# The 32-row substitution of an RWKV-7 mixer: its matrix moved to PSUM, its products laid along contiguous rows

## Chip, cores and metric

The kernel runs on 1 core of one Trainium2 chip. The metric is device microseconds of one execution, the median of several runs.

## The reference

A decoder trunk of two layers over 512 tokens of width 1024. Layer 0 mixes its tokens with an RWKV-7 recurrence (8 heads of 64) beside a spatial gate, layer 1 with latent attention; each then attends to 256 memory tokens and passes through a mixture of 32 experts. Only the recurrence matters here:

```python
def rwkv7_recurrence(r, w, k, v, kk, a):
    def step(state, inp):
        r_t, w_t, k_t, v_t, kk_t, a_t = inp
        sa = jnp.einsum('bhvk,bhk->bhv', state, -kk_t)
        state = (state * w_t[:, :, None, :]
                 + sa[..., None] * (kk_t * a_t)[:, :, None, :]
                 + v_t[..., None] * k_t[:, :, None, :])
        return state, jnp.einsum('bhvk,bhk->bhv', state, r_t)
    ...
    _, y = lax.scan(step, state0, xs)
```

The kernel computes it in chunks of 128 tokens. Within a chunk the steps are a triangular system with a unit diagonal, and its 128x128 matrix has to be inverted: 4 chunks times 8 heads give 32 such matrices.

## The kernel before, in words

`mixer` (L717) holds layer 0's mixer. Two generators share its first part. `prep` (L831) makes the matrices and inverts them. `filler` (L991) runs the projections that need no inverse: `take_g`, `take_r`, `shifted` into `vv`, and `spatial`. The lines after them advance the two in turn, and a scheduler then fixes the order on each engine; every engine works through its own queue in that order.

A projection (`proj_cm`, `proj_tm`; lines L212 to L214) is a row of 128x512 matmuls in three passes, since each operand is split into a high and a low part: ACT casts the high part (L218), POOL subtracts the low part (L219). Its sum in PSUM is picked up by `shifted` (L760 on ACT, then L761 on DVE, which frees the PSUM tile), and for `take_r` by a product `bt` (L941 on DVE) that feeds the small matmuls `pbn` (L946).

In `prep`, PE makes all 32 matrices (L871) and ACT copies them to `Aab` (L873). The four 32x32 blocks of each diagonal are inverted together, on DVE alone. Partition 32x+u holds, for block x, row u, and the free axis the 32 matrices:

1. L877 copies the diagonal blocks into `tsum`, transposed in the free axis and multiplied by a triangular mask; four instructions, one per block of 32 partitions. L878 transposes them in 32x32 blocks into `dd`.
2. L881 to L883, for i from 1 to 31, is the substitution: 31 dependent pairs, a product of i by i elements and a sum along its last axis. Row i of the inverse `tr` comes from all rows before it.

```python
for i in range(1, 32):
    V.tensor_tensor(prod[:, 0:i, 0:i], tr[:, 0:i, 0:i].rearrange("p j c -> p c j"),
                    dd[:, None, 0:i, i].to_broadcast([P, i, i]), op=ALU.mult)
    V.tensor_reduce(tr[:, i, 0:i], prod[:, 0:i, 0:i], axis=AX.X, op=ALU.add)
```

   `tr`, `prod` and `dd` have rows of 32 elements, 128 bytes. The product reads `tr` down its columns, 128 bytes from element to element, and `dd` as well; it writes `prod` with the summed index last, so the sum reads contiguous elements.
3. L890 and L892 transpose the result into `TT` (in the tile `h`) and `tsum`, while L887 copies it on ACT. PE then joins the blocks to 64 and to 128 rows (`pC` L900, `pT` L910, and L922 to L931), with ACT and DVE copies between.

The loop yields at every second step, so DVE's queue holds `r`, `bt`, `bon` and four `vv` of the filler between the pairs. All of this uses one PSUM pool with four tiles of tag "a" (prep) and four of tag "b" (filler). When both generators are done the second part of the mixer runs chunk by chunk, then cross attention, then the experts, whose weights come from HBM through SP's queue (L104).

Of the kernel before, what the change touches and what calls it, by code (L numbers as in the profile page):

```python
# [15 lines left out]
ALU = mybir.AluOpType  # L16
AX = mybir.AxisListType
# [3 lines left out]
P = 128  # L21
# [323 lines left out]
def out_proj(k, pool, sp, w, yh, yl, gb, tags="ab", order=(0, 1), route=False, fine=False):  # L345

    nc = k.nc
    V = nc.vector
    st = [k.ln_stats(pool, i) for i in range(NT)]
    for half in range(2):  # L350
        s = slice(half * 512, (half + 1) * 512)

        def consume(i, ps):
            V.scalar_tensor_tensor(k.h[:, i, s], k.h[:, i, s], ALPHA, ps, op0=ALU.mult, op1=ALU.add)
            V.bn_stats(st[i][:, half], k.h[:, i, s])
            if half == 1:
                scale = k.ln_scale(pool, st[i], f"ln_{i}")
                if route:
                    k.router.step(i, scale, *gb)
                else:  # L360
                    k.layer_norm(k.h[:, i, :], scale, *gb)

        yield from proj_tm(k, sp, w, half * 512, yh, yl, NT, tags[half], consume, by_token=(half == 1), order=order, fine=fine)
# [353 lines left out]
def mixer(k):  # L717
    nc, tc, A, c = k.nc, k.tc, k.A, k.cst
    V, S_, G_, E = nc.vector, nc.scalar, nc.gpsimd, nc.tensor
# [4 lines left out]
    with ExitStack() as st:  # L724
# [18 lines left out]
        with ExitStack() as s1:  # L743
# [3 lines left out]
            xh = pool.tile([P, KD, T], F32R, name="xh")  # L747
            xl = pool.tile([P, KD, T], F32R, name="xl")
            mt1 = pool.tile([P, MIXA.shape[1]], F32, name="mixa")
            scan, selT, tri, dmask, sel = (mt1[:, o:o + n] for o, n in ((0, 512), (512, 512), (1024, P), (1152, 32), (1184, 2)))  # L750
            omu = pool.tile([P, 14], F32, name="omu")
            oka = pool.tile([P, 4], F32, name="oka")
            wa = pool.tile([P, T], F32, name="wa", tag="wa")
# [77 lines left out]
            def prep():  # L831
# [24 lines left out]
                Aab = pool.tile([P, 32, P], F32, name="Aab")  # L856
                b8 = pool.tile([P, 2048], F32, name="b8")
                t8 = pool.tile([P, 2048], F32, name="t8")
                tsum, dd = (b8[:, o:o + 1024].rearrange("p (i u) -> p i u", u=32) for o in (0, 1024))
                tr, prod = (t8[:, o:o + 1024].rearrange("p (i u) -> p i u", u=32) for o in (0, 1024))  # L860
                G_.memset(tr, 0.0)
                G_.memset(t8[:, 0:1024:33], 1.0)
                for x in range(1, 4):
                    G_.memset(TT[32 * x:32 * x + 32, 0:32 * x, :], 0.0)
                for p in range(4):
                    pj = [k.psum("a", name="pab") for j in range(2)]
                    for q in range(NT):
                        qs = slice(q * P, (q + 1) * P)
                        for j in range(2):
                            r = slice(64 * j, 64 * j + 64)  # L870
# [3 lines left out]
                    yield  # L874
                for x in range(4):
                    r = slice(32 * x, 32 * x + 32)
                    V.tensor_tensor(tsum[r].rearrange("p i u -> p u i"), Aab[r, :, r], dmask[r, None, :].to_broadcast([32, 32, 32]), op=ALU.mult)  # L877
                V.transpose(b8[:, 1024:], b8[:, 0:1024])  # L878
                yield
                for i in range(1, 32):  # L880
                    V.tensor_tensor(prod[:, 0:i, 0:i], tr[:, 0:i, 0:i].rearrange("p j c -> p c j"),  # L881
                                    dd[:, None, 0:i, i].to_broadcast([P, i, i]), op=ALU.mult)
                    V.tensor_reduce(tr[:, i, 0:i], prod[:, 0:i, 0:i], axis=AX.X, op=ALU.add)  # L883
                    if i % 2:
                        yield

                S_.copy(prod, tr.rearrange("p i c -> p c i"))  # L887
                for x in range(4):
                    r = slice(32 * x, 32 * x + 32)
# [5 lines left out]
                for n in range(2):  # L895
                    ps = k.psum("a", name="pC")
                    for u in range(16):
                        for h in (0, 64):
                            r, ri = slice(h + 32, h + 64), slice(h, h + 32)
# [91 lines left out]
            def filler():  # L991
# [3 lines left out]
                yield from spatial()  # L995

            pr, fl = prep(), filler()
            next(pr)
            for n in (2, 2, 2, 2):
# [11 lines left out]
        with ExitStack() as s2:  # L1011
# [146 lines left out]
            op = out_proj(k, tp, sp, A["ab_w_out"], y, None, ln, tags="aa", order=(1, 0), fine=True)  # L1158
# [895 lines left out]
def build(nc, tc, A, out, phases):  # L2054
    k = B(nc, tc, A, out)
    with ExitStack() as st:
# [18 lines left out]
        for ph in phases:  # L2075
# [17 lines left out]
            elif ph[0] == "xamoe":  # L2093
                with ExitStack() as rs:
                    cross_attention(k, ph[1], rs)
                    fill = None
                    if ph[1] == 0:
                        fill = early_keys(k, 1, "g")
                    moe(k, rs, ph[1], ph[2], fill)
            elif ph[0] == "xa":  # L2100
                with ExitStack() as rs:
                    cross_attention(k, ph[1], rs)
            elif ph[0] == "mix":
                mixer(k)
            elif ph[0] == "mla":
                mla(k)
            elif ph[0] == "store":
                if k.kept:
                    k.kept.close()
                nc.sync.dma_start(out.rearrange("(i p) d -> p i d", p=P), k.h)  # L2110
# [40 lines left out]
```

## Time and profile before

| | us |
|---|---|
| median of 3 runs (1974.23 to 1977.72) | 1976.72 |
| the profiled execution | 1979.66 |
| its span, first to last instruction | 1977.9 |

The profiled execution is 2.9 us above the median, and 1.8 us of it lie outside the span. PE is busy for 91% of the span, DVE for 48%, ACT for 27%, POOL for 14%. "Busy" adds up instructions; an idle stretch of an engine is printed in square brackets at the instruction that ended it, with the engine, tile and line that released it.

### The profile page before, as it was taken

The numbers are of one execution on the slowest core, as the hardware profiler recorded it, in microseconds if no ns is written. First come the engines' busy times: TensorE is split into PE (matmuls) and PEld (weight loads), VectorE is DVE, ScalarE is ACT, GpSimd is POOL, SyncE is SP. The second block draws the span as 40 slices with busy tenths as digits, with TensorE's granted clock in tenths as the row PEclk, the third lists the DMA queues.
The fourth block names the chain that finished last, engine by engine and source line by source line (L and its number), as shares of the span: only waits on it lengthen the run. The fifth ranks groups of instructions, "written<-read, shape, count | busy, mean of one in ns | idle before, by whom it ended". The sixth has DMA issues, their size and how long they took to land. (4 is left out here: it accounts for less than half of the span.)

```text
span 1977.9 us, 23921 instructions
## 1 busy us (share of the span) xinstructions
PE 1799.2 (91%) x9222; PEld 1105.9 (56%) x9222; DVE 956.1 (48%) x2129; ACT 530.0 (27%) x992; POOL 280.4 (14%) x278
## 2 busy tenths in 40 slices
PE   8778998999979999999896999999979999998895
PEld 5567877878844344434336866678863334433332
DVE  5686456855553233323236566575573233333325
ACT  6313313344221111111122555434322111111110
POOL 3532433410110000000022100130020000000002
PEclk9886889999979999999998999999989999999998
DMA  5220105472889999999995200234679999999992
GB/s 187 65 64 23 54 1 203 128 234 78 330 311 414 420 419 419 420 420 419 420 369 171 88 22 22 86 112 155 227 311 360 420 419 419 420 420 420 421 418 102
DMA packets 126022, 514.69 MB, mean 260 GB/s; under 512 B 15520, under 2 KB 49472, under 8 KB 77264
## 3 DMA queue, kind: packets, MB, share of 16 engines
q1 hardware_dynamic: 115152, 486.60, 62.3%
q0 software_dynamic: 7056, 18.12, 2.8%
q10 hardware_dynamic: 3696, 8.41, 1.1%
q8 instruction: 74, 1.21, 0.2%
q14 instruction: 44, 0.36, 0.1%
HBM read 506.19 MB, written 14.70 MB: 263 GB/s over the span
## 5 line engine op out<-in xcount | busy, mean ns | idle before, releaser
L1756 PE MATMUL pu<-wu,xT 128*64 128x512 f32 x1024 | 240.7, 594 | 21.9 <-DMA wu<-in_moe_w_up_dram 21.8
L1756 PE MATMUL pg<-wg,xT 128*64 128x512 f32 x1024 | 232.8, 601 | 1.6 <-DMA wg<-in_moe_w_gate_dram 1.6
L1782 PE MATMUL py<-wd,hh 128*64 128x512 f32 x1024 | 230.4, 599 | 0.0
L1789 DVE SCALAR_TENSOR_TENSOR wy<-py,tab,wy 128x512 fp32r<-128x512 f32 x64 | 45.5, 747 | 285.7 <-ACT wy L1788 285.4
L1762 DVE TENSOR_TENSOR hh<-hh,pu 128x512 f32<-128x512 f32 x32 | 22.0, 688 | 322.0 <-PE pu L1756 322.0
L1756 PEld LDWEIGHTS pu<-wu,xT 128*64 128x64 f32 x1024 | 77.4, 137 | 178.1 <-issue 131.3
L1796 PE MATMUL pc<-wy,wc 128*128 128x512 f32 x480 | 139.8, 422 | 27.3 <-DVE h L1806 27.3
L1745 ACT ACTIVATE xT<-px,ch 128x128 f32<-128x128 f32 x128 | 48.2, 457 | 424.7 <-PE px L1738 404.2
L1756 PEld LDWEIGHTS pg<-wg,xT 128*64 128x64 f32 x1024 | 77.6, 139 | 149.4 <-issue 130.6
L1806 DVE TENSOR_TENSOR h<-h,pc 128x512 f32<-128x512 f32 x240 | 151.0, 680 | 8.6 <-PE pc L1796 8.6
L1782 PEld LDWEIGHTS py<-wd,hh 128*64 128x64 f32 x1024 | 71.4, 138 | 135.1 <-issue 130.5
L1796 PEld LDWEIGHTS pc<-wy,wc 128*128 128x128 f32 x480 | 81.6, 189 | 85.9 <-DVE h L1806 50.0
L1720 POOL DMA_INDIRECT xg<-rows,idx x32 | 33.5, 1046 | 532.6 <-PE px L1738 513.2
L1726 ACT ACTIVATE xg<-xg 128x1024 f32<-128x1024 f32 x32 | 39.7, 1240 | 245.4 <-DMA xg<-rows,idx 245.4
L218 ACT CAST wh<-wt 128x1024 fp32r<-128x1024 f32 x50 | 51.8, 1050 | 107.1 <-PE ptm L214 61.5
L219 DVE TENSOR_TENSOR wl<-wt,wh 128x1024 fp32r<-128x1024 f32 x37 | 47.9, 1302 | 58.4 <-ACT wh L218 57.9
L212 PE MATMUL ptm<-wh,oh 128*128 128x512 f32 x192 | 75.6, 394 | 0.0
L213 PE MATMUL ptm<-wl,oh 128*128 128x512 f32 x192 | 75.0, 391 | 0.0
L214 PE MATMUL ptm<-wh,ol 128*128 128x512 f32 x192 | 75.0, 390 | 0.0
L212 PE MATMUL pcm<-xh,wh 128*128 128x512 f32 x144 | 61.7, 429 | 7.6 <-ACT xh L218 7.2
L214 PE MATMUL pcm<-xh,wl 128*128 128x512 f32 x144 | 60.5, 420 | 0.5 <-DVE wl L219 0.5
L213 PE MATMUL pcm<-xl,wh 128*128 128x512 f32 x144 | 60.0, 416 | 0.2 <-DVE xl L219 0.2
(565 smaller groups left out, 3432.1 us busy)
## 6 DMA issues: line engine op xcount, KB each, us to landing
wg<-in_moe_w_gate_dram SPq DMA_DIRECT2D x128, 1024.0 KB, 19.8
wu<-in_moe_w_up_dram SPq DMA_DIRECT2D x128, 1024.0 KB, 20.2
wd<-in_moe_w_down_dram SPq DMA_DIRECT2D x124, 1024.0 KB, 19.9
wr<-in_ab_w_in_dram SPq DMA_DIRECT2D x8, 1024.0 KB, 5.7
wr<-in_xa_wkv_dram SPq DMA_DIRECT2D x8, 1024.0 KB, 10.8
wt<-in_xa_wkv_dram SPq DMA_DIRECT2D x8, 1024.0 KB
wr<-in_xa_wq_dram SPq DMA_DIRECT2D x8, 1024.0 KB, 8.2
wt<-in_xa_wo_dram SPq DMA_DIRECT2D x8, 1024.0 KB
```

The lines of the kernel that those rows point to most:

```text
L212: nc.tensor.matmul(out, lh, rh, start=start, stop=False)
L213: nc.tensor.matmul(out, lh, rl, start=False, stop=False)
L214: nc.tensor.matmul(out, ll, rh, start=False, stop=stop)
L218: k.nc.scalar.copy(hi, src)
L219: (eng or k.low()).tensor_tensor(lo, src, hi.bitcast(F32), op=ALU.subtract)
L1726: self.k.nc.scalar.activation(x[:, :D], x[:, :D], AF.Identity, scale=x[:, D:D + 1], bias=x[:, D + 1:D + 2])
L1745: r = nc.scalar.activation(self.xT[:, kk, :], pk, AF.Identity, scale=gk, bias=bk)
L1756: nc.tensor.matmul(ps[j * M:(j + 1) * M, :], self.xT[:, half * 4 + kk, j * M:(j + 1) * M], w[j][:, kk, :], start=(half == 0 and kk == 0), ...
L1782: nc.tensor.matmul(py[n][j * M:(j + 1) * M, :], self.hT[:, half * 2 + kk, j * M:(j + 1) * M], w[j][:, kk, n * 512:(n + 1) * 512], start=(h ...
L1789: nc.vector.scalar_tensor_tensor(yl, py[n], self.tab()[:, 1:2], yh.bitcast(F32), op0=ALU.mult, op1=ALU.subtract)
L1796: self.k.nc.tensor.matmul(ps, self.C[:, i * P:(i + 1) * P], y, start=start and not last, stop=last)
L1806: k.nc.vector.tensor_add(k.h[:, i, s], k.h[:, i, s], pc)
```

## The change

The substitution keeps its arithmetic and changes its layout. `dd` moves to PSUM: two ACT copies (L883 of the new file) fill the tiles `pd`, 16 rows of each matrix in each. The product now walks `tr` and `prod` along their rows, with the factor from PSUM repeated along a row; the sum reads `prod` down its columns. Since the two halves lie in two tiles, from step 17 on the product takes two instructions: rows 0 to 15, of which only columns 0 to 15 are computed, and rows 16 to i-1. The elements skipped are zero, so `prod` is set to zero once. The mask is left out, because the loop never reads what it cleared; of the four copies that carried it two stay on DVE and two go to ACT.

```diff
-                tsum, dd = (b8[:, o:o + 1024].rearrange("p (i u) -> p i u", u=32) for o in (0, 1024))
+                tsum = b8[:, 0:1024].rearrange("p (i u) -> p i u", u=32)
...
+                G_.memset(prod, 0.0)
...
-                    V.tensor_tensor(tsum[r].rearrange("p i u -> p u i"), Aab[r, :, r], dmask[r, None, :].to_broadcast([32, 32, 32]), op=ALU.mult)
+                    (V.tensor_copy if x < 2 else S_.copy)(tsum[r].rearrange("p i u -> p u i"), Aab[r, :, r])
                 V.transpose(b8[:, 1024:], b8[:, 0:1024])
+
+                dp = [k.psum("a", name=f"pd{n}") for n in range(2)]
+                for n in range(2):
+                    S_.copy(dp[n], b8[:, 1024 + n * 512:1536 + n * 512])
+                dp = [t.rearrange("p (i u) -> p i u", u=32) for t in dp]
                 yield
                 for i in range(1, 32):
-                    V.tensor_tensor(prod[:, 0:i, 0:i], tr[:, 0:i, 0:i].rearrange("p j c -> p c j"),
-                                    dd[:, None, 0:i, i].to_broadcast([P, i, i]), op=ALU.mult)
-                    V.tensor_reduce(tr[:, i, 0:i], prod[:, 0:i, 0:i], axis=AX.X, op=ALU.add)
+                    n = min(i, 16)
+                    V.tensor_tensor(prod[:, 0:n, 0:n], tr[:, 0:n, 0:n], dp[0][:, 0:n, i, None].to_broadcast([P, n, n]), op=ALU.mult)
+                    if i > 16:
+                        V.tensor_tensor(prod[:, 16:i, 0:i], tr[:, 16:i, 0:i],
+                                        dp[1][:, 0:i - 16, i, None].to_broadcast([P, i - 16, i]), op=ALU.mult)
+                    V.tensor_reduce(tr[:, i, 0:i], prod[:, 0:i, 0:i].rearrange("p j c -> p c j"), axis=AX.X, op=ALU.add)
```

The scheduler also moves the filler's instructions a little. DVE's queue at the head of the substitution, before (`t` holds `tr` and `prod`, `b` holds `dd`):

```order
L877 TENSOR_TENSOR b_560<-Aab,mixa 32x32x32 x4
L878 STREAM_TRANSPOSE b_560<-b_560 128x1024
L881 TENSOR_TENSOR t_561<-t_561,b_560 128x1
L761 SCALAR_TENSOR_TENSOR r<-pcm,cv,r 128x511
L883 TENSOR_REDUCE t_561<-t_561 128x1
L941 SCALAR_TENSOR_TENSOR bt<-r,cv,yb 128x512
L881 TENSOR_TENSOR t_561<-t_561,b_560 128x2x2
```

and of the change, somewhat later in the queue, where the same filler instructions now stand (lines after L878 bear higher numbers, L941 is L951):

```order
L889 TENSOR_TENSOR t_561<-t_561,pd_702 128x5x5
L893 TENSOR_REDUCE t_561<-t_561 128x5
L889 TENSOR_TENSOR t_561<-t_561,pd_702 128x6x6
L761 SCALAR_TENSOR_TENSOR r<-pcm,cv,r 128x511
L893 TENSOR_REDUCE t_561<-t_561 128x6
L951 SCALAR_TENSOR_TENSOR bt<-r,cv,yb 128x512
L889 TENSOR_TENSOR t_561<-t_561,pd_702 128x7x7
```

`r` and `bt` now stand behind five whole steps of the substitution. ACT's queue at the same place, as a piece of the difference:

```order
-L873 COPY Aab<-pab 128x4x128 x4
+L874 COPY Aab<-pab 128x4x128 x4
+L878 COPY b_560<-Aab 32x32x32 x2
+L883 COPY pd_702<-b_560 128x512
+L883 COPY pd_703<-b_560 128x512
 L218 CAST wh<-wr 128x1024
 L760 ACTIVATE r<-pcm,omu 128x512
```

Four copies now stand ahead of the cast and of the `r` that DVE's `bt` waits for. PE's queue differs at one place, where the blocks are joined (`pC`, L910 in the new file): its first two matmuls stand two projection matmuls earlier, and one projection matmul that stood ahead of the other 62 stands behind the `pN` that follow.

## Rows read from the trace of the kernel before

**Rows 1.** The page: span, and part 1, busy time of the engines.

```profile
span 1977.9 us, 23921 instructions
...
PE 1799.2 (91%) x9222; PEld 1105.9 (56%) x9222; DVE 956.1 (48%) x2129; ACT 530.0 (27%) x992; POOL 280.4 (14%) x278
```

**Rows 2.** Windows: stretch and length, busy PE, PEld, DVE, ACT, POOL, clock, DMA, GB/s.

```profile
100.00:150.00 50.00, 38.36 (x152) 30.41 (x151) 43.93 (x62) 9.26 (x12) 14.88 (x6) 0.84 0.20 63
...
176.00:234.00 58.00, 57.68 (x552) 50.07 (x552) 21.27 (x74) 20.77 (x27) 10.99 (x6) 0.72 0.09 28
...
500.00:1000.00 500.00, 460.88 (x2151) 218.03 (x2152) 185.84 (x452) 85.47 (x148) 28.60 (x51) 0.98 0.97 399
```

**Rows 3.** Timeline of PE, 114 to 172 us: start, duration, instruction, [idle before, releaser].

```profile
114.83 1.87 PE L946 MATMUL pbn<-mixa,bt 128*128 128x2 f32 x8 [4.12 <-DVE bt L941]
...
143.64 0.50 PE L212 MATMUL ptm<-wh,xh 128*128 128x512 f32 x1 [3.81 <-DVE vv L761]
...
149.97 0.79 PE L212 MATMUL ptm<-wh,xh 128*128 128x512 f32 x1 [3.71 <-DVE vv L761]
...
171.70 0.41 PE L900 MATMUL pC<-h,Aab 32*32 32x32 f32 x4 [5.60 <-DVE h L890]
```

**Rows 4.** Groups of DVE, 100 to 175 us: count, busy us, mean ns, idle before.

```profile
L881 DVE TENSOR_TENSOR t<-t,b 128x1 f32<-128x1 f32 (+30 forms) x31 | 32.8, 1059 | 1.0
L883 DVE TENSOR_REDUCE t<-t 128x1 f32<-128x1 f32 (+30 forms) x31 | 15.6, 502 | 0.9
```

**Rows 5.** Timeline of DVE, 101 to 203 us.

```profile
101.87 8.26 DVE L877 TENSOR_TENSOR b<-Aab,mixa 32x1024 f32<-32x1024 f32 x4 [3.07 <-ACT Aab L873]
...
111.45 0.79 DVE L881 TENSOR_TENSOR t<-t,b 128x1 f32<-128x1 f32 x1
...
114.70 0.15 DVE L881 TENSOR_TENSOR t<-t,b 128x4 f32<-128x4 f32 x1
...
116.74 0.19 DVE L948 COPY bon<-pbn 128x32 f32<-128x32 f32 x1 [1.49 <-PE pbn L946]
...
122.28 0.75 DVE L761 SCALAR_TENSOR_TENSOR vv<-pcm,cv,vv 128x511 f32<-128x511 f32 x1 [1.11 <-ACT vv L760]
...
127.68 2.44 DVE L881 TENSOR_TENSOR t<-t,b 128x256 f32<-128x256 f32 x1
...
130.61 0.70 DVE L881 TENSOR_TENSOR t<-t,b 128x289 f32<-128x289 f32 x1
...
166.12 1.80 DVE L881 TENSOR_TENSOR t<-t,b 128x961 f32<-128x961 f32 x1
167.96 1.15 DVE L883 TENSOR_REDUCE t<-t 128x31 f32<-128x961 f32 x1
169.15 5.04 DVE L890 STREAM_TRANSPOSE h<-t 32x1024 f32<-32x1024 f32 x4
...
201.61 1.37 DVE L975 TENSOR_SCALAR z<-z,zmv,zry 128x128 f32<-128x128 f32 x5
```

**Rows 6.** Timeline of POOL, 121 to 130 us.

```profile
121.74 2.41 POOL L219 TENSOR_TENSOR wl<-wr,wh 128x1024 fp32r<-128x1024 f32 x1 [7.50 <-ACT wh L218]
127.23 2.40 POOL L219 TENSOR_TENSOR wl<-wr,wh 128x1024 fp32r<-128x1024 f32 x1 [3.08 <-ACT wh L218]
```

**Rows 7.** Groups of DVE by form, 0 to 240 us.

```profile
L975 DVE TENSOR_SCALAR z<-z,zmv,zry 128x128 f32<-128x128 f32 x16 | 4.7, 338 | 0.0
...
L985 DVE TENSOR_TENSOR yb<-pz,bs 128x512 f32<-128x512 f32 x4 | 2.8, 691 | 16.9 <-PE pz L984 16.9
...
L976 DVE TENSOR_TENSOR z<-z,zg 128x512 f32<-128x512 f32 x4 | 2.7, 684 | 0.0
```

**Rows 8.** Groups of ACT by form, 0 to 300 us.

```profile
L218 ACT CAST wh<-wr 128x1024 fp32r<-128x1024 f32 x18 | 18.7, 1041 | 62.4 <-PE pcm L213 38.9 <-issue 17.8 <-DMA wr<-in_ab_w_in_dram 5.7
L218 ACT CAST xh<-h 128x512 fp32r<-128x512 f32 x8 | 4.6, 617 | 0.9 <-DMA h<-in_xT_dram 0.9
...
L887 ACT COPY t<-t 128x1024 f32<-128x1024 f32 x1 | 1.9, 1943 | 8.9 <-DVE t L883 8.9
```

**Rows 9.** Waits of SP's DMA queue, 85 to 520 us: total, times, longest.

```profile
SPq L584 <- PE pcm L214: 54.8, 1, 54.8
```

More of the change, by code (lines that the diff above doesn't have):

```diff
@@ L749, in mixer @@
             mt1 = pool.tile([P, MIXA.shape[1]], F32, name="mixa")
-            scan, selT, tri, dmask, sel = (mt1[:, o:o + n] for o, n in ((0, 512), (512, 512), (1024, P), (1152, 32), (1184, 2)))
+            scan, selT, tri, _, sel = (mt1[:, o:o + n] for o, n in ((0, 512), (512, 512), (1024, P), (1152, 32), (1184, 2)))
             omu = pool.tile([P, 14], F32, name="omu")
```

## The prediction

> **What bounds the kernel now.** I read the page first: PE is busy for 91% of the span and DVE for 48% [rows 1], so a DVE edit pays only where PE waits for DVE. The windows show where that can be. In the expert stage (500 to 1000 us) the DMA share is 0.97: nothing on DVE matters there. From 100 to 150 us DVE is busy for 43.9 of 50 us, PE for 38.4, and DMA is at 0.20 [rows 2]. This is the substitution. PE's timeline names four stops there, and DVE ends all of them: 4.12 us for `bt`, 3.81 and 3.71 us for two `vv` that sit in DVE's queue between products, and 5.60 us for the transposed result `h` [rows 3]: 17.2 us of idle PE. After it PE works for 57.7 of 58 us [rows 2], so what PE gains by 171.70 us it keeps. Nothing later is due at a fixed time: SP's first expert load stands behind a wait of 54.8 us for PE's projections [rows 9], so the weight stream starts earlier by as much.
>
> The end of the substitution is the end of its last sum, 167.96 + 1.15 = 169.11 us [rows 5]; the first `pC` follows 2.6 us later, after two transposes of 1.26 us [rows 3, 5].
>
> **How DVE's time splits.** The 31 products take 32.8 us, the 31 sums 15.6 us [rows 4]. The fixed part of a small one is 0.15 us (2x2 elements). The sum of 961 contiguous elements takes 1.15 us, 1.04 ns an element; the product of 961, both inputs 128 bytes apart, 1.80 us, 1.72 ns; of 289, 0.70 us, 1.9 ns [rows 5]. All steps together have 1+4+...+961 = 10416 elements. At 1.85 ns and 0.15 us a piece the products should take 23.9 us; 9 us are missing. Products far above the line show where: the one of 256 elements takes 2.44 us where 0.62 fit, while POOL's subtraction runs from 127.23 to 129.63 us [rows 5, 6]; seven such products carry the 9 us. At 122.28 us L761, with one input in PSUM, takes its usual 0.75 us under POOL's subtraction of 121.74 to 124.15 us [rows 5, 6]. One PSUM input takes an instruction out of that conflict.
>
> **The change, part by part.**
>
> *Copies.* Before: 8.26 us on DVE from 101.87 us, a transpose, first product at 111.45 us [rows 5]. After: two copies on DVE beside two on ACT. They write 128 bytes apart, as L877 does; at its 2.07 us each DVE takes 4.1 us. ACT's copy with such steps on its reading side takes 1.94 us [rows 8], two make 3.9. Should a DVE copy without a second input be faster, down to nothing, ACT decides, and the end is 105.7 us; I take 105.9. Transpose 1.3 us, then one `pd` copy on ACT: 0.62 us by the 128x512 cast [rows 8]. The first product starts at 107.9 us: **-3.6 us**. The second `pd` copy is not needed before step 17.
>
> *Products.* The first 16 steps have 1496 elements, the later ones 15 x 256 + 3160 = 7000: 8496 in all. `tr` and `prod` are now contiguous along a row, so I take 1.04 ns: 8.8 us. Fixed: 31 x 0.15 = 4.65 us. A second product does not wait for the first; five independent L975 take 1.37 us where five single ones would be 1.69, so 0.08 us of a follower is hidden [rows 5, 7], and with a gap I take 0.1 x 15 = 1.5 us. Sum 15.0 us in place of 32.8: **-17.8 us**, of which 9 is POOL's conflict. A PSUM input costs nothing by itself in the rows: L985 with one takes 691 ns, L976 without 684 [rows 7]; 46 x 7 ns = 0.3 us. Bounds: nothing by itself, up to the old 1.85 ns, which would add 6.9 us.
>
> By the Trainium skill ("VectorE: DVE Perf Modes", section "The TRN2 errata") a VectorE operation that reads PSUM carries a fixed 120 cycles against 58 from SBUF; at its 0.96 GHz that is 65 ns, and over 46 products my estimate from that page is 3.0 us against this change. The rows differ by 7 ns, and I go by them.
>
> *Sums.* They now read 128 bytes apart. No DVE row before has a sum like that. The lower bound is the contiguous 1.04 ns, the upper one the product's 1.72 to 1.9 ns with two such streams. The nearest single stream is ACT's L887, 1.94 us against 1.04 us for a contiguous cast of the same size [rows 8], and on the writing side L877 with 1.9 ns. Both say that one stream is enough, so 1.8 ns: 31 x 0.15 + 10416 x 1.8 ns = 23.4 us in place of 15.6: **+7.9 us**.
>
> The Trainium skill ("SBUF — State Buffer", section "Door 1: The DMA port swizzle") says SBUF is read in lines of 16 bytes and each step to a new line pays a penalty. It gives no price. It speaks against a sum that keeps 1.04 ns, and so against my first rival.
>
> *DVE's other waits.* Idle time behind PE and ACT was 1.49 us (`bon`) and 1.11 us (first `vv`) [rows 5]. PE reaches these tiles only about 2 us earlier, so I leave 2.5 us in place, plus 0.5 us for 15 more gaps. End of the substitution: 107.9 + (169.11 - 111.45) - 17.8 + 7.9 + 0.5 = 156.2 us, **12.9 us earlier**.
>
> *PE's side.* `bt` stands behind five small steps (11 x 0.2 us) and behind ACT's two `pd` copies, a cast and `r`: it ends near 112.8 us, so the first stop shrinks from 4.1 to about 2 us. PE then comes to the second stop at 137.6 us; its `vv` now stands behind product 22 and is done near 134, so that stop goes. Six matmuls later the fourth `vv`, behind sum 25, is done near 140.9 us: some 2 us of the third stop stay. PE needs 15.7 us from there (171.70 - 149.97 - 5.60 = 16.1, less two matmuls) and is at `pC` at 156.6 us; `h` is ready at 156.2 + 2.6 = 158.8. So DVE still decides, the last stop keeps 2.2 us, and `pC` starts 12.9 us earlier. One more projection matmul between the first `pC` and the rest costs 0.4 us. Gain 12.5 us.
>
> Free edits: the new memset stands among POOL's first instructions, long before its tile is used. ACT's cast comes 1 us later, covered by the 2 us that PE still stands at `pbn`; without that cover it would cost the 1 us. The two `pd` tiles hold half of tag "a", which has no other user until `pC`.
>
> *Sum.* 1979.66 - 12.5 = 1967.2 us for the profiled execution; the median lies 2.9 us lower: **1964.2 us**. I leave out a better clock: it was granted at 0.84 around the stops and 0.72 in the joining stage [rows 2], and shorter stops may lift it, for 1 to 3 us more.
>
> **Rivals.**
>
> 1. *The sum does not slow down* (1.04 ns). For: the DVE may hide a step that ACT cannot. Against: L877. The substitution ends 7.9 us sooner, near 148.5; the third stop goes too, and PE itself decides, at `pC` near 153.5: gain 18 us, **1959 us**, 1956 with a better clock.
>
> 2. *The product does not get faster*: the repeated PSUM read costs what the strides did (+6.9 us), or POOL's conflict stays (+9). For: no row has such a repeated operand. Against: L985 and L761 above. The substitution ends at 163 to 165 us, gain 3.5 to 6 us: **1971 to 1973 us**. The page's 3.0 us would leave 9.5, 1967 us. That the change does not do what it says is this case.
>
> 3. *Slower*: the strided sum costs more than two strided streams did. From 3.05 ns an element (1.8 + 12.9 us / 10416) `pC` starts no earlier than before; at 4 ns the substitution ends near 178 us, both `vv` stops return, and the time is 9 us higher, **1986 us**. For: a sum reads and adds in one pass, and nothing in the trace shows one with steps. Against: nothing in the stretch pays over 2 ns without POOL.
>
> **How the numbers follow.** A measurement of this kernel tells some 0.2%, 4 us, from no change. My forecast, with a gain of 9 to 16 us, has 0.60; rival 1, up to 23 us, 0.20; rival 2 has 0.15, a third of it within 4 us; rival 3 has 0.05, most of it slower by over 4 us. Faster 0.90, same 0.06, slower 0.04. The range takes in rival 1 with a better clock and most of rival 2: 1954 to 1972.
>
> **What would show it.** In the new profile: the 46 products near 15 us with none standing out beside POOL; the 31 sums near 23 us, the last at 1.9 us (1.15 if rival 1 holds, over 3 if rival 3 does); first product near 107.9 us; PE's stop for a `vv` gone once and about 2 us once; `pC` near 159 us, still released by `h`; and from there on every stage as long as before. I am wrong if the gain at `pC` does not reach the end, or if the products stay above 20 us.

## The result and the profile after

The changed kernel takes 1962.97 us in the median of 4 runs (1960.93 to 1965.17) against 1975.49 us of the kernel before (4 runs beside it, 1974.23 to 1977.72): a ratio of 0.9931, with a 95% interval of 0.9917 to 0.9946. By the medians that is 12.5 us less, and between 10.7 and 16.4 us by the interval of the ratio. The forecast was 1964.2 us, 12.5 us less than the median of the runs shown.

The profiled execution of the changed kernel took 1962.84 us, at its median; that of the kernel before, 1979.66 us, lies 3 to 4 us above its own. So the two profiles differ by 16.8 us, and what follows accounts for that. The span on the page of the profile and the line of part 1 that answers to [rows 1]:

```profile
span 1961.0 us, 23938 instructions
...
PE 1792.2 (91%) x9222; PEld 1102.1 (56%) x9222; DVE 940.4 (48%) x2142; ACT 535.1 (27%) x996; POOL 278.9 (14%) x279
```

The groups of DVE from 100 to 165 us, beside [rows 4] (line, engine, operation, output<-input, count | busy us, mean ns | idle before):

```profile
L893 DVE TENSOR_REDUCE t<-t 128x1 f32<-128x1 f32 (+30 forms) x31 | 23.8, 766 | 1.0
L889 DVE TENSOR_TENSOR t<-t,pd 128x256 f32<-128x256 f32 (+15 forms) x31 | 10.3, 332 | 1.5 <-ACT pd L883 0.7
L891 DVE TENSOR_TENSOR t<-t,pd 128x17 f32<-128x17 f32 (+14 forms) x15 | 5.5, 367 | 0.0
...
L878 DVE COPY b<-Aab 32x1024 f32<-32x1024 f32 x2 | 2.2, 1087 | 3.0 <-ACT Aab L874 3.0
```

The products fell from 32.8 us to 10.3 + 5.5 = 15.8 us, the sums rose from 15.6 to 23.8 us. DVE's timeline, beside [rows 5], shows where the loop begins and ends:

```profile
106.20 1.25 DVE L879 STREAM_TRANSPOSE b<-b 128x1024 f32<-128x1024 f32 x1 [1.96 <-ACT b L878]
108.10 0.16 DVE L889 TENSOR_TENSOR t<-t,pd 128x1 f32<-128x1 f32 x1 [0.66 <-ACT pd L883]
...
113.81 0.19 DVE L958 COPY bon<-pbn 128x32 f32<-128x32 f32 x1 [0.76 <-PE pbn L956]
...
124.29 0.42 DVE L889 TENSOR_TENSOR t<-t,pd 128x256 f32<-128x256 f32 x1
...
152.06 0.42 DVE L889 TENSOR_TENSOR t<-t,pd 128x256 f32<-128x256 f32 x1
152.40 0.63 DVE L891 TENSOR_TENSOR t<-t,pd 128x465 f32<-128x465 f32 x1
153.06 1.76 DVE L893 TENSOR_REDUCE t<-t 128x31 f32<-128x961 f32 x1
```

The substitution now ends at 153.06 + 1.76 = 154.82 us, where it ended at 169.11 us. The second product starts 0.08 us before the first one ends (152.06 + 0.42 = 152.48 against 152.40). The product at 124.29 us takes 0.42 us, like the one at 152.06 us, although POOL reads SBUF all the while, as POOL's timeline says:

```profile
124.21 2.41 POOL L219 TENSOR_TENSOR wl<-wr,wh 128x1024 fp32r<-128x1024 f32 x1 [3.06 <-ACT wh L218]
```

Before, such a product took 2.44 us [rows 5, 6]. PE's timeline, beside [rows 3], with the first matmul of the part that follows the joining stage (`ptv`, the last row):

```profile
112.72 1.05 PE L956 MATMUL pbn<-mixa,bt 128*128 128x2 f32 x8 [1.72 <-DVE bt L951]
...
139.60 0.50 PE L212 MATMUL ptm<-wh,xh 128*128 128x512 f32 x1 [1.42 <-DVE vv L761]
...
157.41 0.39 PE L910 MATMUL pC<-h,Aab 32*32 32x32 f32 x4 [4.12 <-DVE h L900]
...
218.09 0.60 PE L1052 MATMUL ptv<-cst,vv 128*128 128x128 f32 x4
```

and the same matmul of the kernel before:

```profile
233.72 0.60 PE L1042 MATMUL ptv<-cst,vv 128*128 128x128 f32 x4
```

`pC` starts 171.70 - 157.41 = 14.3 us earlier, and `ptv` 15.6 us. In both kernels `pC` starts 2.6 us after the last sum of the substitution and waits for it, so these 14.3 us are those by which DVE's substitution ends earlier. On PE's side the stops are 1.72 + 1.42 + 4.12 = 7.3 us, where they were 17.2 us: 10.0 us saved. Of the other 4.3 us, 0.5 us are two projection matmuls that now run behind `pC` (0.23 us apart at a clock of 1.00). PE came to the first stop 0.3 us later, so 4.1 us are left, and they are PE's clock. Windows of the kernel before (stretch and length, busy PE with its matmuls, granted clock, DMA share, GB/s): behind its first stop, across its two `vv` stops, and behind `pC`:

```profile
115.00:121.00 6.00, 6.00 (x20) 0.57 0.29 114
...
143.60:150.00 6.40, 2.65 (x7) 0.53 0.23 82
150.00:157.00 7.00, 7.00 (x22) 0.70 0.00 0
...
172.00:180.00 8.00, 8.00 (x150) 0.50 0.01 2
180.00:200.00 20.00, 19.68 (x235) 0.50 0.08 17
```

The changed kernel behind its first stop, behind its `vv` stop, and behind `pC`:

```profile
112.70:118.00 5.30, 5.28 (x20) 0.68 0.61 198
...
139.60:146.00 6.40, 6.40 (x28) 1.00 0.41 141
...
157.40:162.00 4.60, 4.59 (x22) 0.63 0.02 4
162.00:172.00 10.00, 9.68 (x275) 0.65 0.02 3
172.00:180.00 8.00, 8.00 (x46) 0.59 0.00 0
```

A clock of 0.50 is the lower of TensorE's two levels (1.2 of 2.4 GHz). After the stops of 3.81 and 3.71 us it was granted at 0.53 (a window that takes in the second stop) and 0.70; after the one of 1.42 us it stayed at 1.00. Up to `pC`, which DVE releases, a better clock can help the time only where DVE waits for PE, as for `pbn`: otherwise PE just comes earlier to `pC` and waits longer. From `pC` to `ptv` it counts in full: that stretch takes 60.7 us in place of 62.0, 1.3 us less, at a mean clock of 0.78 in place of 0.70, although it holds the two matmuls more. From `ptv` to the end of the span both kernels take nearly the same time: 1977.9 - 233.72 = 1744.2 us and 1961.0 - 218.09 = 1742.9 us.

### The profile page after: what moved, and what is told of

Read it like the earlier page. It is cut to its first block, busy times and chain, and to the rows that moved or that the text cites. A ratio compares the mean times of both kernels' runs of the same rounds, so it can differ in the third digit from the quotient of the medians.

```text
span 1961.0 us, 23938 instructions
## 1 busy us (share of the span) xinstructions
PE 1792.2 (91%) x9222; PEld 1102.1 (56%) x9222; DVE 940.4 (48%) x2142; ACT 535.1 (27%) x996; POOL 278.9 (14%) x279
## 5 line engine op out<-in xcount | busy, mean ns | idle before, releaser
L218 ACT CAST wh<-wt 128x1024 fp32r<-128x1024 f32 x50 | 51.8, 1049 | 97.7 <-PE ptm L214 60.7
```

What stands on the lines that cost most here:

```text
L218: k.nc.scalar.copy(hi, src)
```

## Experiments

Three theories stood against each other for where the gain comes from: the products' contiguous rows, the place of the matrix in PSUM (which takes the products out of POOL's way), and the copies at the head. The elements skipped are a fourth part; no run changes them alone. Edits are shown against the changed kernel unless said otherwise, and `...` marks what is left out.

Each edit also changes the order that the scheduler gives to PE's queue. Counted from PE's timelines, 161 projection matmuls stand between `pbn` and the first `pC` in the kernel before and 159 in the change; a different number is given with the run.

**The changed kernel again**, as the measure for the others.

> The changed kernel once more, beside the others of this call, as their base. Theory T (the gain is PE's stops behind DVE: copies 3.3 us earlier, products from 32.8 to 15.8 us, sums from 15.6 to 23.8): 1963 us, ratio 0.9931, first pC near 157.4 us.

Measured: 1962.25 us (1961.9 to 1965.9), ratio 0.9939 (0.9926 to 0.9953). Its profile has stops of 1.34, 0.93 and 4.16 us: the middle one varies by half a microsecond from one execution to the next. `pC` starts at 158.90 us and `ptv` at 220.65 us, 12.8 and 13.1 us earlier than in the kernel before, where the first profile of the change had 14.3 and 15.6 us.

**The old layout, in PSUM.**

```diff
-V.tensor_tensor(prod[:, 0:n, 0:n], tr[:, 0:n, 0:n], dp[0][:, 0:n, i, None]...)
+V.tensor_tensor(prod[:, 0:n, 0:n], tr[:, 0:n, 0:n].rearrange("p j c -> p c j"), dp[0][:, None, 0:n, i]...)
...
-V.tensor_reduce(tr[:, i, 0:i], prod[:, 0:i, 0:i].rearrange("p j c -> p c j"), ...)
+V.tensor_reduce(tr[:, i, 0:i], prod[:, 0:i, 0:i], ...)
```

> Only the layout is put back: products run down the columns of tr and write the summed index last, sums read contiguous elements; the matrix stays in PSUM, split and copies stay. Theory T (PSUM takes the products out of POOL's way; the step of 128 bytes is paid once, in the product or in the sum): products 8496 x 1.85 ns + 6.2 = 21.9 us, sums 15.6 us, so the substitution ends 2 us earlier than with the change (near 152.7 us) and the time is 1 to 3 us below the change. Rival L (the contiguous rows give the gain): products go back above 28 us and the time rises by 6 us or more against the change.

Measured: 1961.57 us (1956.69 to 1963.34), ratio 0.9927 (0.9913 to 0.9941). DVE's groups:

```profile
L893 DVE TENSOR_REDUCE t<-t 128x1 f32<-128x1 f32 (+30 forms) x31 | 15.6, 503 | 1.0
L889 DVE TENSOR_TENSOR t<-t,pd 128x256 f32<-128x256 f32 (+15 forms) x31 | 14.7, 473 | 1.5 <-ACT pd L883 0.7
L891 DVE TENSOR_TENSOR t<-t,pd 128x17 f32<-128x17 f32 (+14 forms) x15 | 8.0, 535 | 0.0
```

Products and sums together take 38.3 us, in the change 39.6 us. The theory is right and its rival falls: turning the layout moves the 128-byte steps from the product's reads to the sum's, and is worth nothing; if anything, the old layout is better: the last sum ends at 153.21 us, 1.6 us earlier than in the change, and the median is 0.7 us lower.

**The new layout, without PSUM.**

```diff
-dp = [k.psum("a", name=f"pd{n}") for n in range(2)]
-for n in range(2):
-    S_.copy(dp[n], b8[:, 1024 + n * 512:1536 + n * 512])
-dp = [t.rearrange("p (i u) -> p i u", u=32) for t in dp]
+dp = [b8[:, 1024 + n * 512:1536 + n * 512].rearrange("p (i u) -> p i u", u=32) for n in range(2)]
```

> Only the matrix is put back into SBUF: the two PSUM copies go, the rest of the change stays. Theory T: products have two SBUF inputs again and are held up wherever POOL's subtraction runs, seven times for 4 to 9 us together; first product 1.4 us earlier, substitution ends near 157 to 162 us, time 3 to 8 us above the change. Rival L: products stay at 15 to 16 us, time 0 to 2 us below the change, since a copy is saved.

Measured: 1974.98 us (11 runs, 1973.46 to 1977.72), ratio 1.0002 (0.9993 to 1.0011): the whole gain is gone, though not by PSUM alone, as shown below. DVE's group of the first products, and two products of its timeline, the second one while POOL reads (its row is the last):

```profile
L886 DVE TENSOR_TENSOR t<-t,b 128x256 f32<-128x256 f32 (+15 forms) x31 | 19.0, 612 | 1.0
```

```profile
127.31 0.42 DVE L886 TENSOR_TENSOR t<-t,b 128x256 f32<-128x256 f32 x1
...
128.68 2.29 DVE L886 TENSOR_TENSOR t<-t,b 128x256 f32<-128x256 f32 x1
```

```profile
128.29 2.40 POOL L219 TENSOR_TENSOR wl<-wr,wh 128x1024 fp32r<-128x1024 f32 x1 [3.22 <-ACT wh L218]
```

The same instruction on the same shape takes 0.42 us beside nothing and 2.29 us beside POOL. The products as a whole take 8.7 us more than in the change (19.0 + 5.5 against 10.3 + 5.5). The Trainium skill ("SBUF — State Buffer", section "Who interferes with whom") has the rule: a VectorE instruction with two SBUF inputs contends with a GpSimd instruction that reads SBUF, one with a single SBUF input, outside the modes that use both ports, doesn't. These rows agree, and the timeline gives the price: it is about what is left of POOL's instruction. Four products that start within 0.4 us of its start pay 1.9 to 2.0 us, two that start later in it 0.5 and 0.3 us.

The theory had the mechanism, but forecast 3 to 8 us, and 12.7 us came. PE's timeline:

```profile
115.54 1.87 PE L953 MATMUL pbn<-mixa,bt 128*128 128x2 f32 x8 [3.89 <-DVE bt L948]
...
144.32 0.50 PE L212 MATMUL ptm<-wh,xh 128*128 128x512 f32 x1 [3.42 <-DVE vv L761]
...
151.44 0.80 PE L212 MATMUL ptm<-wh,xh 128*128 128x512 f32 x1 [5.23 <-DVE vv L761]
...
166.55 0.42 PE L907 MATMUL pC<-h,Aab 32*32 32x32 f32 x4 [2.79 <-DVE h L897]
```

All four stops are back, 15.3 us in all. `pC` starts 9.1 us later than in the change, as the substitution ends that much later (163.97 against 154.82 us), and `ptv` 13.9 us later (232.03 us). The difference has a second cause: only 144 projection matmuls stand ahead of `pC` here, 15 fewer than in the change, and these run behind it. Ahead of `pC` they could have filled its stop of 2.79 us. So by estimate some 3 of the 12.7 us are the order's; a run with PE's order kept was not made.

**The sum over contiguous elements** (the price of the sum's steps; it adds over the wrong index, so the kernel no longer computes the reference).

```diff
-V.tensor_reduce(tr[:, i, 0:i], prod[:, 0:i, 0:i].rearrange("p j c -> p c j"), ...)
+V.tensor_reduce(tr[:, i, 0:i], prod[:, 0:i, 0:i], ...)
```

> The sums read the products in the order in which they lie (they add over the wrong index; nothing else is changed), so that only their step of 128 bytes goes. Theory T (DVE still decides at pC): sums 15.6 us instead of 23.8, substitution ends near 147 us, PE's 1.4 us stop for vv goes and pC starts near 151.7 us, when PE gets there: 5.7 us, with a better clock up to 9 us below the change. Rival P (after the change PE decides, DVE has slack): within 2 us of the change.

Measured: 1955.67 us (1952.02 to 1956.66), ratio 0.9907 (0.9892 to 0.9922), 6.6 us below the change. The last sum of DVE's timeline, then PE's first `pC`, which no longer waits:

```profile
145.43 1.15 DVE L893 TENSOR_REDUCE t<-t 128x31 f32<-128x961 f32 x1
```

```profile
149.92 0.39 PE L910 MATMUL pC<-h,Aab 32*32 32x32 f32 x4
```

So in the change DVE still decided, as the theory said; PE decides here, where the substitution ends at 146.58 us.

**The masked copies back on DVE.**

```diff
-(V.tensor_copy if x < 2 else S_.copy)(tsum[r].rearrange("p i u -> p u i"), Aab[r, :, r])
+V.tensor_tensor(tsum[r].rearrange("p i u -> p u i"), Aab[r, :, r], dmask[r, None, :].to_broadcast([32, 32, 32]), op=ALU.mult)
```

> Only the four copies are put back: with the mask, all on DVE. PSUM, split and layout stay (the scheduler puts pC further back in PE's queue). Theory T: the first product starts 4 us later (near 112 us), the substitution ends near 158.5 us, bt is back near 114.8 us; time 3 to 6 us above the change. Rival C (the copies lie beside other work): within 1.5 us of the change.

Measured: 1963.97 us (1959.5 to 1966.93), ratio 0.9936 (0.9922 to 0.995): not to be told from the change. DVE's group of the copies and PE's stop at `pC`:

```profile
L878 DVE TENSOR_TENSOR b<-Aab,mixa 32x1024 f32<-32x1024 f32 x4 | 8.2, 2056 | 2.7 <-ACT Aab L874 2.7
```

```profile
162.01 0.42 PE L910 MATMUL pC<-h,Aab 32*32 32x32 f32 x4 [5.26 <-DVE h L900]
```

The first product starts at 111.54 us and the substitution ends at 159.42 us, as the theory had it, but the time doesn't follow. The rival has the time right and the reason wrong: the copies do hold DVE up. `pC` comes 4.6 us later than in the change but `ptv` (220.01 us) only 1.9 us, since the scheduler put ten filler matmuls ahead of `pC` that stood behind it (169 in place of 159). A delay ahead of `pC` costs what the filler can't cover.

**The kernel before with the matrix in PSUM and nothing else**: masked copies, old layout, no element skipped (the product is in two pieces from step 17, since the matrix lies in two tiles).

```diff
 # against the kernel before
...
-V.tensor_tensor(prod[:, 0:i, 0:i], tr[:, 0:i, 0:i].rearrange("p j c -> p c j"), dd[:, None, 0:i, i]...)
+V.tensor_tensor(prod[:, 0:i, 0:n], tr[:, 0:n, 0:i].rearrange("p j c -> p c j"), dp[0][:, None, 0:n, i]...)
+if i > 16:
+    V.tensor_tensor(prod[:, 0:i, 16:i], tr[:, 16:i, 0:i].rearrange("p j c -> p c j"), dp[1][:, None, 0:i - 16, i]...)
```

> The kernel before with one thing changed, the matrix in PSUM: masked copies on DVE, old layout, no element skipped; the product is in two pieces from step 17 on because the matrix lies in two tiles. Theory T: products 10416 x 1.85 ns + 6.2 = 25.4 us instead of 32.8, first product 1.3 us later, substitution ends near 163 us: 6 us less of stops for PE, with the clock 6 to 9 us below the kernel before. Rival L (the gain needs the new layout or the skipped elements): 3 us or less below the kernel before.

Measured: 1964.78 us (1963.62 to 1966.13), ratio 0.9943 (0.993 to 0.9956), 11.3 us below the kernel before by the ratio. DVE's products, its last sum, and PE's `pC` and `ptv`:

```profile
L889 DVE TENSOR_TENSOR t<-t,pd 128x1 f32<-128x1 f32 (+30 forms) x31 | 18.2, 589 | 1.0
...
L891 DVE TENSOR_TENSOR t<-t,pd 128x17 f32<-128x17 f32 (+14 forms) x15 | 8.0, 532 | 0.0
```

```profile
161.01 1.16 DVE L893 TENSOR_REDUCE t<-t 128x31 f32<-128x961 f32 x1
```

```profile
164.76 0.42 PE L910 MATMUL pC<-h,Aab 32*32 32x32 f32 x4 [5.52 <-DVE h L900]
...
220.71 0.60 PE L1052 MATMUL ptv<-cst,vv 128*128 128x128 f32 x4
```

Products 26.2 us, sums 15.6 us, end of the substitution 162.17 us, as the theory had them. The gain was put at 6 to 9 us and came out larger, and the rows show where: `pC` starts 6.9 us earlier than in the kernel before, `ptv` 13.0 us. The scheduler put 178 projection matmuls ahead of `pC`, 17 more than before. They fill 17 x 0.23 = 3.9 us in which PE would have waited for DVE. By this estimate some 7 of the 11.3 us are PSUM's, and the rest is the order's.

**Sums split too, three copies on DVE, and the blocks that `pC` reads first transposed first.**

```diff
-(V.tensor_copy if x < 2 else S_.copy)(...)
+(V.tensor_copy if x < 3 else S_.copy)(...)
...
-V.tensor_reduce(tr[:, i, 0:i], prod[:, 0:i, 0:i]..., ...)
+if i > 16:
+    V.tensor_reduce(tr[:, i, 16:i], prod[:, 16:i, 16:i]..., ...)
+V.tensor_reduce(tr[:, i, 0:n], prod[:, 0:i, 0:n]..., ...)
...
-for x in range(4):
+for x in (1, 3, 0, 2):
```

> A version that may beat both: the change with its sums also split from step 17 on (8496 elements instead of 10416), three of the four copies on DVE and one on ACT, and the transposes into h in the order 1, 3, 0, 2, since pC reads blocks 1 and 3 first. Theory T: copies end 0.85 us earlier, sums near 21.5 us, substitution ends 2.5 us earlier (near 152 us) and h is there 1.26 us sooner after it; PE's three stops together 7.3 to some 4.5 us; 3 to 5 us below the change, near 1958 to 1960 us. Rival P (PE's remaining stops are not DVE's): no difference.

Measured: 1961.19 us (1959.83 to 1963.07), ratio 0.9924 (0.9912 to 0.9937): 1 to 2 us below the change, with intervals that overlap, so not shown to be faster. The sums fell to 22.5 us and `pC` starts at 152.76 us, but the scheduler moved it ahead of ten filler matmuls (149 in place of 159), and a stop of 3.34 us is left there.

**The steps in the product's write.** The change's plain copies write 128 bytes apart at full speed (1.09 us for 1024 elements, above). If a product could do that too, neither it nor the sum would pay.

```diff
-V.tensor_tensor(prod[:, 0:n, 0:n], tr[:, 0:n, 0:n], dp[0][:, 0:n, i, None]...)
+V.tensor_tensor(prod[:, 0:n, 0:n].rearrange("p c j -> p j c"), tr[:, 0:n, 0:n], dp[0][:, 0:n, i, None]...)
...
-V.tensor_reduce(tr[:, i, 0:i], prod[:, 0:i, 0:i].rearrange("p j c -> p c j"), ...)
+V.tensor_reduce(tr[:, i, 0:i], prod[:, 0:i, 0:i], ...)
```

> The changed kernel, but the product reads along contiguous rows and writes its result 128 bytes apart, so that the sum reads contiguous elements again; the result is the same. Theory T: a step of 128 bytes has to be paid in a read, not in a write of a VectorE operation with one input in PSUM, as in the changed kernel's two plain copies, which write 128 bytes apart and take 1.09 us for 1024 elements. Then the products stay near 16 us, the sums fall to 15.6 us, the substitution ends near 147 us, pC starts without a wait for the transposed result, and the time is 5 to 8 us below the changed kernel's: 1955 to 1958 us, as with the sum over the wrong index. Rival R: a write with steps costs what a read with steps costs, as the masked copy of the kernel before (2.07 us for 1024) would have it. Then the products take 22 to 23 us, the sums 15.6 us, the end is near 153 us, and the time is that of the changed kernel or 1 us less: 1961 to 1963 us.

Measured: 1961.59 us (1957.33 to 1963.12), ratio 0.9912 (0.9891 to 0.9933). DVE's groups:

```profile
L893 DVE TENSOR_REDUCE t<-t 128x1 f32<-128x1 f32 (+30 forms) x31 | 15.6, 503 | 1.0
L889 DVE TENSOR_TENSOR t<-t,pd 128x256 f32<-128x256 f32 (+15 forms) x31 | 14.8, 477 | 1.5 <-ACT pd L883 0.7
L891 DVE TENSOR_TENSOR t<-t,pd 128x17 f32<-128x17 f32 (+14 forms) x15 | 8.5, 564 | 0.0
```

and one product from its timeline, which with contiguous rows took 0.42 us:

```profile
148.98 0.63 DVE L889 TENSOR_TENSOR t<-t,pd 128x256 f32<-128x256 f32 x1
```

The theory falls, its rival is right. The steps cost the same in all three places: 38.3 us with them in the product's reads, 38.9 in its write, 39.6 in the sum's reads.

**The same, with the copies and the order of the transposes of the experiment that splits the sums.**

> The kernel with the product that writes with steps, and besides three of the four copies on VectorE and one on ScalarE, and the transposes of the result in the order 1, 3, 0, 2 (the blocks that the first pC reads come first). Theory T: PE is the engine that decides once the substitution ends near 147 us, so starting 0.8 us sooner and transposing in another order gains at most 1 us over the kernel with the stepped write alone: 1954 to 1957 us. Rival R (a write with steps costs what a read does): VectorE still decides, and the two edits gain their 0.8 us and up to 2 us of transposes: 1958 to 1961 us.

Measured: 1959.98 us (1957.06 to 1961.59), ratio 0.9908 (0.9888 to 0.9927). With the rival right above, its 1958 to 1961 us is right here. Here 154 projection matmuls stand ahead of `pC`. This is the lowest time of a kernel that computes the reference, 2 to 3 us below the change; the intervals overlap.

## Why the prediction was right

**What bounds the kernel.** Right. DVE pays here only where PE waits for it; what was gained at `pC` was kept to the end, and SP's first expert load waits 55.6 us behind the projections, where it waited 54.8 us [rows 9]. That DVE still decides after the change was shown by the contiguous sum.

**Copies** (-3.6 us). Right in sum: the first product starts at 108.10 us, forecast 107.9. DVE's price was wrong: 1.09 us each, not the masked copy's 2.07 us. That cost nothing, since ACT's pair (4.12 us, forecast 3.9) ends last and DVE's transpose waits 1.96 us for it. But the time need not show the term: with the masked copies back the substitution ended 4.6 us later, and by another order of PE's queue the time could not be told from the change.

**Products** (15.0 us). Right: 15.8 us, with 0.08 us of each of the 15 second ones beside the first, so 14.6 us of the queue's time. POOL's conflict is gone, and PSUM costs nothing in itself: a product of one element takes 0.16 us, and 0.16 us as well in the experiment without PSUM. The sentence on the 65 ns of the Trainium skill ("VectorE: DVE Perf Modes", section "The TRN2 errata") is not borne out here.

**Sums** (23.4 us). Right: 23.8 us, 1.7 ns an element in the last one ((1.76 - 0.15) us over 961). The rule of the Trainium skill on lines of 16 bytes ("SBUF — State Buffer", section "Door 1: The DMA port swizzle") agrees with these sums, but not with the two plain copies, whose steps in the write cost nothing that can be seen (1.09 us for 1024 elements). Rival 1 falls. Rivals 2 and 3 fall with the two sums above.

**End of the substitution** (156.2 us). It came at 154.82 us. The forecast left DVE's idle time in place, but the wait for `pbn` halved, 0.76 us for 1.49 [rows 5]: behind a shorter stop those eight matmuls took 1.05 us instead of 1.87 [rows 3]. That is 0.7 of the 1.4 us. The 0.4 us that the products took less are balanced by the 0.4 us that the sums took more; the rest was not followed up.

**PE's stops.** The first (forecast about 2 us, measured 1.72) and the `vv` stops (one gone, one of 2 us; measured one of 1.42) are right. The last was put at 2.2 us and measured 4.12: PE reached `pC` at 157.41 - 4.12 = 153.3 us, not at 156.6. The 15.7 us from the third stop to `pC` were taken from the kernel before, where the matmuls behind the stop ran at a clock of 0.70; after a stop of 1.42 us they ran at 1.00 and took 13.7 us. This error cost the forecast nothing, since `pC` waits for DVE, and only made the stop longer.

**What it missed.** `pC` gained 14.3 us where 12.9 were forecast, the 1.4 us by which the substitution ended earlier. Behind `pC` the forecast had a loss of 0.4 us for the moved matmul, and a gain of 1.3 us came: 1.7 us, which is the better clock that the sum leaves out ("for 1 to 3 us more"). Together that is the difference between 12.5 and 15.6 us.

**The total.** The right median is thus partly luck. Between the two profiles the mixer gained 15.6 us, not 12.5; in the medians it is 12.5 us, since the profiled execution of the kernel before lay 3 to 4 us above its median. In the second profile of the change it was 13.1 us, so such a difference between two profiles can be off by 2 to 3 us. How the clock stood around the stops in a median execution stays open: the kernel before has only this one trace.

**What the parts are worth.** The prediction's own terms say that the layout is worth nothing: it saves 6.9 us in the products (its bound "up to the old 1.85 ns") and costs 7.9 us in the sums. It gave 9 us to POOL's conflict. The end of the substitution, ahead of everything that PE's order can hide, shows the shares: of its 14.3 us PSUM alone brings 169.11 - 162.17 = 6.9 us (9.1 us where it is taken out of the change), the copies 159.42 - 154.82 = 4.6 us and the layout -1.6 us. The rest, 4.4 us, falls to the skipped elements by subtraction; products of 26.2 us with PSUM alone against 14.7 + 8.0 = 22.7 us in the old layout in PSUM show 3.5 us of it. In time the shares can't be read off. PSUM alone measured 11.3 of the change's 12.5 us, but by estimate some 7 us without the 17 matmuls that the scheduler moved ahead of `pC`, and without PSUM the rest measured nothing, but some 3 us by estimate with the change's order. So PSUM is the largest part and not nearly all of it. As no run kept PE's order fixed, the shares of the time stay estimates.

## What to carry to other kernels

Where a VectorE product with two SBUF inputs runs beside a GpSimd operation that reads SBUF, look for instances that take several times the line through the others, and move one input to PSUM before turning any layout. A layout that moves a step from one instruction to the next saves nothing: add up both. Before a difference in time is put down to an edit, count what the scheduler moved on the engine that bounds the kernel: here 10 to 17 matmuls changed sides, and hid or doubled what DVE had gained. Behind a stop of PE look at the granted clock, but a faster PE gains nothing where it then waits for the same DVE result.

## What the runs showed that was not expected

- A plain VectorE copy writes 128 bytes apart for 1.09 us per 1024 elements; the masked copy (a tensor_tensor) takes 2.06 us, and a product with one input in PSUM and the same step in its write 0.63 us for 256 elements against 0.42 us without. Which part of the instruction makes the copy exempt was not tried.
- The sums of the experiment without PSUM took 23.4 us, no more than in the change: they didn't pay for POOL, only products with two SBUF inputs did.
- Stops of PE differ in what follows them: 1.42 us ahead of a projection matmul left the clock at 1.00, while 1.72 us ahead of the small `pbn` matmuls was followed by 0.68. Other profiles show that both count. Behind stops of 1.34 and 1.49 us ahead of `pbn` (the change again, the old layout in PSUM) the clock was 0.71 and 0.66 over the next 4.6 us, and behind stops of 0.82 us ahead of the same `pbn` (contiguous sums, steps in the write) it was 1.00.
